# Last layer's down projection with activations stationary and 512 weight columns moving, post-norm and output with tokens on the partitions

## The chip, the cores and the metric

The kernel runs on one core of a Trainium2 chip. The metric is the time of one execution on the device in microseconds. A core has five engines that run side by side: TensorE (PE; PEld is its loading of the stationary operand), VectorE (DVE), ScalarE (ACT), GpSimd (POOL) and SyncE (SP), which here issues most of the DMA transfers. A matmul keeps a stationary 128x128 operand in the array and streams the columns of a moving operand past it.

## The reference, cut to what matters

A trunk of two layers over 16 learned meta tokens and 512 tokens of width 1024. Layer 0 mixes with attention, layer 1 with a gated DeltaNet; each is followed by a feed-forward stage. In each stage the input is normalised before, and the result is normalised again before it is added to the residual:

```python
def conv_ffn(h, w_up, conv_w, w_down):
    u = causal_dwconv(h @ w_up, conv_w)
    gate, up = jnp.split(u, [FFN_DIM], axis=-1)
    return (jax.nn.gelu(gate, approximate=True) * up) @ w_down
...
        f = conv_ffn(rmsnorm(h, norm_ffn_pre[i]), ffn_w_up[i], ffn_conv[i], ffn_w_down[i])
        h = h + rmsnorm(f, norm_ffn_post[i])
    return h[:, N_META:]
```

`rmsnorm` divides a token's row by the root of its mean square and multiplies by a gain per feature. FFN_DIM is 2816, so the down projection is 2816 by 1024; of its result only the 512 tokens are returned.

## The kernel before, in words

**Layout.** Everything lies transposed: features on the partitions (1024 features are KT = 8 tiles of 128), tokens along the free dimension. Tokens are cut in two halves; by layer 1's FFN they are 260 (the last 4 meta tokens and 256 tokens) and 256. The residual is `h[half]`, a tile of 128 x 8 x tokens.

**Precision.** Each product is computed from operands split in a high and a low part: `xh*wh + xl*wh + xh*wl`, three matmuls for each 128x128 tile of weights, accumulated in PSUM. This is `dense` (L300): the weight tile is stationary, the tokens of one half move past it, with 260 or 256 columns.

**Weights.** They come in units (`_units`, L65) laid out in DRAM in the order of use. `load` (L274) fetches a unit (at most 128 x 1024 floats) by a DMA on SP into one of two staging tiles, ACT casts it to `wh` (L285), DVE subtracts to get `wl` (L292). There are eight pairs `wh`/`wl` in this stage: six in pool `wp`, and two in `wx` for every fourth unit. `need(u)` (L295) loads units up to one ahead of `u`.

**Order.** `push(u, fn)` runs unit `u` for half 0 at once and puts half 1 off: up to six calls stay in `pending` (the lag, L1417), and the oldest is popped as a new one is pushed. `flush` runs what is left. A compile-time scheduler lays out each engine's order from these calls and modelled durations; each engine then runs its own order strictly, waiting on semaphores.

**The FFN** (`ffn`, L770) goes through 22 feature tiles of the hidden layer in blocks of FB = 7, 7, 8. An up unit makes `conv_tile` (L737): 24 matmuls, a multiplication by the pre-norm's factor (L748), three taps of the causal convolution (L755 on ACT, L764 on DVE); a gate unit adds GELU (L786), an up unit the product and its split in `ah` and `al` (L794 to L796). After a block and four units of the next, eight down units follow (`down`, L799), one for each tile of 128 output features: FB[b] x 3 matmuls for each half, and the result is copied (b = 0, on ACT) or added (L811, on DVE) to `m[half]`.

**The end.** In the last block each tile of `m` is squared on ACT (L352) and added on POOL to a running tile (L353). After the eighth, matmuls with a column of 1/D sum over the partitions (L342), DVE adds epsilon (L361), POOL takes the power -1/2 (L363), PE spreads the factors over the partitions (L365) and ACT copies them (L367). `boundary` (L402) then makes `m * gain * factor` (L411) and adds it to `h` (L412) for eight feature tiles, and a DMA on SP stores each tile (L418). Half 0 does this while half 1's last tiles run on PE; half 1 does it at the end.

Of the kernel before, what the change touches and what calls it, by code (L numbers as in the profile page):

```python
# [9 lines left out]
F32 = mybir.dt.float32  # L10
F32R = mybir.dt.float32r
BF16 = mybir.dt.bfloat16
AF = mybir.ActivationFunctionType
ALU = mybir.AluOpType
# [3 lines left out]
P = 128  # L18
D = 1024
KT = 8  # L20
NM = 16
SEQ = 512
# [4 lines left out]
FB = (7, 7, 8)  # L27
# [13 lines left out]
EPS = 1e-6  # L41
# [23 lines left out]
def _units():  # L65
    u = []
    def add(mat, layer, r0, nk, c0, M):
        u.append((mat, layer, r0, nk, c0, M))
    add("attn_w_in", 0, 0, 8, 4096, 16)
    for m in range(8):  # L70
        for s in range(4):
            add("attn_w_in", 0, 0, 8, s * 1024 + m * 128, 128)
    for m in range(8):
        add("attn_w_out", 0, 0, 8, m * 128, 128)
    def ffn(layer):
        def up(b):
            r = []
            for j in range(FB[b]):
                jj = sum(FB[:b]) + j
                r.append(("ffn_w_up", layer, 0, 8, jj * 128, 128))  # L80
                r.append(("ffn_w_up", layer, 0, 8, 2816 + jj * 128, 128))
            return r
        def down(b):
            return [("ffn_w_down", layer, sum(FB[:b]) * 128, FB[b], m * 128, 128) for m in range(8)]
        u.extend(up(0))
        for b in (1, 2):
            x = up(b)
            u.extend(x[:4]); u.extend(down(b - 1)); u.extend(x[4:])
        u.extend(down(2))
    ffn(0)  # L90
    add("dn_w_in", 0, 0, 8, -1, 40)
    for kind, g in DNSEQ:
        for hl in range(NG):
            if kind == "P":
                add("dn_w_out", 0, 0, 4, (NG * g + hl) * 128, 128)
                continue
            add("dn_w_in", 0, 0, 8, {"Q": 0, "K": 1024, "V": 2048, "H": 3072}[kind] + (NG * g + hl) * 128, 128)
    for m in range(8):
        add("dn_w_out", 0, 512, 4, m * 128, 128)
    ffn(1)  # L100
    return u


@with_exitstack
def trunk(ctx, tc, h0, wflat, params, out):
    nc = tc.nc
    pc = _param_layout()
    units = _units()
# [3 lines left out]
    HALF = [(0, 272), (272, 256)]  # L112
# [5 lines left out]
    sm = ctx.enter_context(tc.tile_pool(name="sm", bufs=1))  # L118
# [251 lines left out]
    def new_x(half, name):  # L370
        return take(half, name, F32R)


    def prenorm_tile(half, k, name, layer, xh, xl, ss):
        ss.add(h[half][:, k, :], tmp2)
        g = ng(name, layer, k)
        nc.scalar.activation(xh[:, k, :], h[half][:, k, :], AF.Identity, scale=g)
        nc.vector.scalar_tensor_tensor(xl[:, k, :], h[half][:, k, :], g, xh[:, k, :].bitcast(F32), op0=ALU.mult, op1=ALU.subtract)  # L378
# [23 lines left out]
    def boundary(half, m, ssm, post, pre):  # L402
        r = ssm.inv()
        n = HALF[half][1]
        last = pre is None
        if not last:
            xh, xl = new_x(half, "xh"), new_x(half, "xl")
            ss = SumSq(half)
        for k in range(KT):
            t = tmp2("bt")  # L410
            nc.vector.scalar_tensor_tensor(t[:, :n], m[:, k, :], ng(post[0], post[1], k), r[:, :n], op0=ALU.mult, op1=ALU.mult)  # L411
            nc.vector.tensor_tensor(h[half][:, k, :], h[half][:, k, :], t[:, :n], op=ALU.add)  # L412
            if not last:
                prenorm_tile(half, k, pre[0], pre[1], xh, xl, ss)
            else:
                s = max(HALF[half][0], NM)
                e = HALF[half][0] + n
                nc.sync.dma_start(out[:, k, s - NM:e - NM], h[half][:, k, s - HALF[half][0]:n])  # L418
        if not last:
            X[half] = (xh, xl, ss.inv())  # L420


    pending = []
# [346 lines left out]
    def ffn(layer, post, pre):  # L770
        with ExitStack() as cx:
            fp = cx.enter_context(tc.tile_pool(name="fp", bufs=1, reuse_waits="tile"))
            acts = {}
            m = [None, None]
            ssm = [None, None]
            carry = {}

            def conv(u, half, ft):
                return conv_tile(u, half, ft, 3, pc["ffn_conv"] + layer * 132, 44, fp, carry)

            gates = {}

            def gate(u, half, j):
                cv = conv(u, half, j)
                g = fp.tile([P, 272], F32, name="gl", tag="gl", bufs=3)[:, :HALF[half][1]]
                nc.scalar.activation(g, cv, AF.Gelu_apprx_tanh)  # L786
                gates[j, half] = g

            def up(u, half, j):
                n = HALF[half][1]  # L790
                cv = conv(u, half, NF + j)
                ah = fp.tile([P, 272], F32R, name="ah", tag=f"ah{half}", bufs=10)[:, :n]
                al = fp.tile([P, 272], F32R, name="al", tag=f"al{half}", bufs=10)[:, :n]
                nc.vector.tensor_tensor(cv, cv, gates.pop((j, half)), op=ALU.mult)  # L794
                nc.scalar.copy(ah, cv)
                nc.vector.tensor_tensor(al, cv, ah.bitcast(F32), op=ALU.subtract)  # L796
                acts[j, half] = (ah, al)

            def down(u, half, b, mt):  # L799
                n = HALF[half][1]  # L800
                j0 = sum(FB[:b])
                if b == 0 and mt == 0:
                    m[half] = take(half, "m")
                if b == 2 and mt == 0:
                    ssm[half] = SumSq(half)
                ps = dense(u, half, lambda k: acts[j0 + k, half][0], lambda k: acts[j0 + k, half][1])
                mm = m[half][:, mt, :]
                if b == 0:
                    nc.scalar.copy(mm, ps)
                else:  # L810
                    nc.vector.tensor_tensor(mm, mm, ps, op=ALU.add)  # L811
                if b == 2:
                    ssm[half].add(mm)
                    if mt == 7:
                        drop(*X[half][:2])
                        boundary(half, m[half], ssm[half], post, pre)
                        drop(m[half])

            def ups(b):
                r = []  # L820
                for j in range(sum(FB[:b]), sum(FB[:b + 1])):
                    r.append(lambda u, half, j=j: gate(u, half, j))
                    r.append(lambda u, half, j=j: up(u, half, j))
                return r

            def downs(b):
                return [lambda u, half, mt=mt: down(u, half, b, mt) for mt in range(8)]

            seq = ups(0)
            for b in (1, 2):  # L830
                x = ups(b)
                seq += x[:4] + downs(b - 1) + x[4:]
            seq += downs(2)
            for f in seq:
                push(nextu(), f)
            flush()
# [602 lines left out]
def _layout(inputs):  # L1439
    f = {k: np.asarray(v) for k, v in inputs.items()}  # L1440
    h = np.concatenate([f["meta_tokens"], f["x"][0]], axis=0).T
    h0 = np.ascontiguousarray(h.reshape(KT, P, T).transpose(1, 0, 2))
    parts = []
    for mat, layer, r0, nk, c0, M in _units():
        if c0 < 0:
            w = np.zeros((D, M), np.float32)
            w[:, 0:8] = f[mat][layer][:, 4096:4104]
            w[:, 32:40] = f[mat][layer][:, 4104:4112]
        else:
            w = f[mat][layer][r0:r0 + nk * P, c0:c0 + M]  # L1450
        parts.append(np.ascontiguousarray(w.reshape(nk, P, M).transpose(1, 0, 2)).reshape(-1))
    wflat = np.concatenate(parts)
    pc = _param_layout()
    prm = np.zeros((P, pc["n"]), np.float32)
    def put(name, a):
        prm[:a.shape[0], pc[name]:pc[name] + a.shape[1]] = a
    for a, b in (("mix_pre", "norm_mix_pre"), ("mix_post", "norm_mix_post"), ("ffn_pre", "norm_ffn_pre"), ("ffn_post", "norm_ffn_post")):
        put(a, f[b].reshape(16, P).T)
    put("gains", np.stack([np.concatenate([f["attn_q_norm"][0]] * 2), np.concatenate([f["attn_k_norm"][0]] * 2), f["dn_o_norm"][0]], axis=1))
    put("bf", f["attn_b_forget"][0][:, None])  # L1460
    prm[32:40, pc["alog"]] = f["dn_a_log"][0]
    prm[32:40, pc["dtb"]] = f["dn_dt_bias"][0]
    put("dn_conv", f["dn_conv"][0].reshape(4 * 24, P).T)
    put("ffn_conv", f["ffn_conv"].reshape(2 * 3 * 44, P).T)
    return {"h0": h0, "wflat": wflat, "params": prm}


# [12 lines left out]
```

## Time and profile before

| what | value |
|---|---|
| median of the runs | 1604.43 us |
| lowest and highest of 3 runs | 1603.03 and 1607.17 us |
| profiled execution: its time | 1601.35 us |
| profiled execution: its span, first to last instruction | 1599.4 us |
| mean granted TensorE clock | 0.977 |
| DMA queue of SP, share of 16 engines | 28.1% |

The span is the stretch from the first to the last instruction on record; the time includes what lies around it. In rows of the timeline, the columns are start in us, duration in us, engine, line, operation, output and inputs with their shape, count, and in brackets the engine's idle time before and what ended it. In rows of groups, busy us and the mean ns of one instruction follow the count. In rows of windows, each engine's busy time stands with its number of instructions, in the order PE, PEld, DVE, ACT, POOL, then the granted clock, the share of DMA and GB/s. Matmuls are pipelined, so a matmul's own duration (about 0.28 us) is longer than the step from one start to the next, which is what PE's time is made of.

### The profile page before, as it was taken

What the parts mean: (1) busy time and instruction counts of PE and PEld (TensorE: products, weight loads), DVE (VectorE), ACT (ScalarE), POOL (GpSimd) and SP (SyncE); (2) the same over time, 40 slices, a digit from 0 to 9 for tenths busy, and PEclk for the clock granted to TensorE, in tenths of its full rate; (3) what the DMA queues carried; (4) which work ended last, traced back from release to release, by engine and by line L of the source; (5) the groups of instructions that cost most, each with busy time, mean ns of one, the idle gap of its engine ahead of it and who ended that gap; (6) DMA issues with size and microseconds to landing.
All of it is one profiled execution on the core that took longest, in us unless ns stands there. A gap on an engine that the chain in (4) does not pass through costs nothing.

```text
span 1599.4 us, 33295 instructions
## 1 busy us (share of the span) xinstructions
PE 1525.8 (95%) x12630; PEld 1486.8 (93%) x12630; DVE 1123.4 (70%) x2629; ACT 815.4 (51%) x1925; POOL 495.8 (31%) x993
## 2 busy tenths in 40 slices
PE   8999999999999999999789899899989999999996
PEld 6999999899999999999789798898989999999996
DVE  7888888948974675674978665676569864765764
ACT  6677777735643442343564456545456543432441
POOL 6434443025300010012556475654154200100112
PEclk9999999999999999999799998999999999999998
DMA  5232222422223222222323322222141323323321
GB/s 175 89 89 79 75 78 85 134 65 82 84 83 100 93 85 88 93 93 72 107 75 90 90 61 71 68 77 61 50 150 66 91 82 106 92 82 106 93 67 53
DMA packets 63327, 139.04 MB, mean 87 GB/s; under 512 B 18584, under 2 KB 31288, under 8 KB 62784
## 3 DMA queue, kind: packets, MB, share of 16 engines
q1 hardware_dynamic: 62544, 134.55, 28.1%
q8 instruction: 99, 1.62, 0.4%
q0 software_dynamic: 480, 2.15, 0.4%
q14 instruction: 60, 0.49, 0.1%
q10 hardware_dynamic: 144, 0.22, 0.0%
HBM read 131.54 MB, written 5.36 MB: 86 GB/s over the span
## 4 chain that ended last, share of the span: by engine, by line
PE 74%; DVE 11%; POOL 5%; DMA 4%; ACT 3%; issue 3%; SPq 1%; POOLq 0%; DVEq 0%; ACTq 0%
PE ps L312 65%; POOL PR L1177 2%; POOL RB L1178 2%; DVE h L412 1%; DVE bt L411 1%; DVE wl L292 1%; PE av L698 1%; DMA w<-wflat 1%; DVE cv L764 1%; DMA gcr<-gcd 1%; PE pt L678 1%; DVE xl L378 1%; ACT wh L285 1%; PE s L1277 1%; DVE qr L577 1%
## 5 line engine op out<-in xcount | busy, mean ns | idle before, releaser
L312 PE MATMUL ps<-xh,wh 128*128 128x256 f32 (+4 forms) x2464 | 717.6, 293 | 16.8 <-DVE ub L748 9.2
L312 PE MATMUL ps<-xl,wh 128*128 128x256 f32 (+4 forms) x2464 | 710.8, 289 | 3.4 <-DVE xl L378 3.0
L312 PE MATMUL ps<-xh,wl 128*128 128x256 f32 (+4 forms) x2464 | 713.6, 290 | 0.0
L312 PEld LDWEIGHTS ps<-xh,wh 128*128 128x128 f32 (+1 forms) x2464 | 469.6, 192 | 22.8 <-DVE ub L748 6.3
L312 PEld LDWEIGHTS ps<-xl,wh 128*128 128x128 f32 (+1 forms) x2464 | 471.1, 191 | 7.4 <-DVE xl L378 4.6
L312 PEld LDWEIGHTS ps<-xh,wl 128*128 128x128 f32 (+1 forms) x2464 | 471.1, 191 | 1.0
L285 ACT CAST wh<-w 128x1024 fp32r<-128x1024 f32 (+3 forms) x226 | 225.1, 997 | 189.5 <-PE ps L312 166.7
L292 DVE TENSOR_TENSOR wl<-w,wh 128x1024 fp32r<-128x1024 f32 (+4 forms) x191 | 220.6, 1156 | 99.3 <-ACT wh L285 98.7
L764 DVE SCALAR_TENSOR_TENSOR cv<-ub,prm,cv 128x256 f32<-128x256 f32 (+2 forms) x494 | 243.8, 498 | 38.4 <-ACT cv L755 29.5
L312 PE MATMUL ps<-ah,wl 128*128 128x256 f32 (+2 forms) x704 | 199.5, 284 | 0.0
L312 PE MATMUL ps<-ah,wh 128*128 128x256 f32 (+2 forms) x704 | 199.3, 283 | 0.0
L312 PE MATMUL ps<-al,wh 128*128 128x256 f32 (+2 forms) x704 | 199.1, 283 | 0.0
L755 ACT ACTIVATE cv<-ub,prm 128x256 f32<-128x256 f32 (+2 forms) x224 | 113.8, 511 | 146.3 <-DVE ub L748 146.2
L748 DVE TENSOR_TENSOR ub<-ps,r 128x256 f32<-128x256 f32 (+2 forms) x224 | 95.4, 428 | 101.5 <-PE ps L312 100.6
L353 POOL TENSOR_TENSOR ssq<-ssq,sq 128x256 f32<-128x256 f32 (+2 forms) x98 | 90.5, 926 | 144.5 <-ACT sq L352 143.0
L312 PEld LDWEIGHTS ps<-ah,wh 128*128 128x128 f32 x704 | 132.6, 189 | 0.0
L312 PEld LDWEIGHTS ps<-al,wh 128*128 128x128 f32 x704 | 132.5, 188 | 0.0
L312 PEld LDWEIGHTS ps<-ah,wl 128*128 128x128 f32 x704 | 132.4, 188 | 0.0
L751 POOL COPY cy<-ub 128x2 f32<-128x2 f32 (+1 forms) x112 | 38.0, 341 | 279.3 <-DVE ub L748 277.7
L292 POOL TENSOR_TENSOR wl<-w,wh 128x512 fp32r<-128x512 f32 x70 | 95.0, 1377 | 72.1 <-ACT wh L285 56.8
L747 POOL COPY ub<-cy 128x2 f32<-128x2 f32 (+1 forms) x112 | 31.3, 280 | 197.1 <-DVE cv L764 160.0
L786 ACT ACTIVATE gl<-cv 128x272 f32<-128x272 f32 (+2 forms) x88 | 36.7, 418 | 42.0 <-DVE cv L764 41.7
(308 smaller groups left out, 2454.5 us busy)
## 6 DMA issues: line engine op xcount, KB each, us to landing
w<-wflat SPq DMA_DIRECT2D x176, 512.0 KB, 3.5
w<-wflat SPq DMA_DIRECT2D x32, 448.0 KB, 3.3
cB<-cdram SPq DMA_DIRECT2D x16, 264.0 KB, 3.3
w<-wflat SPq DMA_DIRECT2D x16, 256.0 KB, 2.7
h<-h SPq DMA_DIRECT2D x8, 272.0 KB, 5.3
cB<-cdram SPq DMA_DIRECT2D x16, 136.0 KB, 3.0
h<-h SPq DMA_DIRECT2D x8, 256.0 KB, 5.0
AB<-dA SPq DMA_DIRECT2D x16, 128.0 KB, 3.2
```

What stands on the lines that cost most here:

```text
L285: nc.scalar.copy(wh[:], w32)
L292: eng.tensor_tensor(wl[:, c], w32[:, c], wh[:, c].bitcast(F32), op=ALU.subtract)
L312: tok(nc.tensor.matmul(o, w[:, a], r[:, c0:c1], start=(i == 0), stop=(i == tot - 1)))
L353: nc.gpsimd.tensor_tensor(self.acc[:, :n], self.acc[:, :n], sq[:, :n], op=ALU.add)
L747: nc.gpsimd.tensor_copy(ub[:, 0:c0], carry.pop(ft)[:, :c0])
L748: nc.vector.tensor_tensor(ub[:, c0:c0 + n], ps, r[:, :n], op=ALU.mult)
L751: nc.gpsimd.tensor_copy(c[:, :c0], ub[:, n:n + c0])
L755: nc.scalar.activation(cv, ub[:, c0:c0 + n], AF.Identity, scale=w[c0])
L764: nc.vector.scalar_tensor_tensor(cv, ub[:, i:i + n], w[i], cv, op0=ALU.mult, op1=ALU.add)
L786: nc.scalar.activation(g, cv, AF.Gelu_apprx_tanh)
L1177: nc.gpsimd.tensor_tensor(t, R3[:, 0:a, l:l + 1].to_broadcast([P, a, w]), A3[:, l:l + 1, l + 1:32].to_broadcast([P, a, w]), op=ALU.mult)
L1178: nc.gpsimd.tensor_tensor(R3[:, 0:a, l + 1:32], R3[:, 0:a, l + 1:32], t, op=ALU.subtract)
```

## The change: what it does

Layer 1's down projection is turned. The activations `ah` and `al` of 128 tokens are stationary, and 512 columns of weights move; the result has tokens on the partitions and output features along the free dimension. The 512 tokens are four blocks of 128 (half 0 drops its 4 meta tokens). Down units hold two rows of tiles by 512 columns; block b has two groups (f = 0 and 1, the two halves of the output features) of four units each, as many units and bytes as before.

`down_rows(b, f)` takes all four units of its group. It pops what is pending, one call after each `need`, so the half-1 calls of the ups are drained ahead of a block's first group; it also loads the four units that follow. Then for each of the four token blocks it runs FB[b] x 3 matmuls of 512 columns into one PSUM bank, and copies (b = 0, ACT) or adds (DVE) it to `m[half]`, now a tile of 128 tokens x 2 x 1024.

In the last block ACT squares the row with a sum along the free dimension (`accum_out`), DVE multiplies by the gain, which a DMA has spread over all partitions from a new input `gpost`; in the first group `turn_h` transposes the residual's block by eight PE transpositions (fp32, 128x128) into two banks, which ACT copies. After the second group DVE adds the two sums and epsilon, POOL takes the power, and DVE makes `m * factor + h` in two pieces of 512 columns, each stored by a DMA of 256 KB. `boundary` loses its last-layer branch, and the output's layout is (128, 4, 1024).

```diff
         def down(b):
+            if layer == 1:
+
+                return [("ffn_w_down", layer, (sum(FB[:b]) + k) * 128, min(2, FB[b] - k), f * 512, 512) for f in range(2) for k in range(0, FB[b], 2)]
             return [("ffn_w_down", layer, sum(FB[:b]) * 128, FB[b], m * 128, 128) for m in range(8)]
...
+            def turn_h(half, tb):
+                if tb == 0:
+                    W["h", half] = take(half, "hT", shape=[P, 2, D])
+                c = HALF[half][1] - 256 + tb * 128
+                for kk in range(2):
+                    pt = psum_tile()
+                    for k in range(4):
+                        nc.tensor.transpose(pt[:, k * 128:k * 128 + 128], h[half][:, kk * 4 + k, c:c + 128], ident[:])
+                    nc.scalar.copy(W["h", half][:, tb, kk * 512:kk * 512 + 512], pt[:])
+
+            def down_rows(b, f):
+                us = [nextu() for _ in range((FB[b] + 1) // 2)]
+                for u in us:
+                    need(u)
+                    if pending:
+                        a, fn = pending.pop(0)
+                        fn(a, 1)
+                while pending:
+                    a, fn = pending.pop(0)
+                    fn(a, 1)
+                    need(us[-1] + 4 - len(pending), 0)
+                need(us[-1] + 4, 0)
+                if b == 0 and f == 0:
+                    for half in range(2):
+                        m[half] = take(half, "m", shape=[P, 2, D])
+                if b == 2 and f == 0:
+                    for half in range(2):
+                        drop(*X[half][:2])
+                    W["g"] = take(0, "gb", shape=[P, D])
+                    nc.sync.dma_start(W["g"][:], gpost[0:1, :].to_broadcast([P, D]))
+                    W["s"] = sm.tile([P, 16], F32, name="rst", tag="rst")
+                fs = slice(f * 512, f * 512 + 512)
+                j0 = sum(FB[:b])
+                for t in range(4):
+                    half, tb = t // 2, t % 2
+                    c = HALF[half][1] - 256 + tb * 128
+                    ps = psum_tile()
+                    for k in range(FB[b]):
+                        wh, wl, nk, M = loaded[us[k // 2]]
+                        a = slice(k % 2 * 512, k % 2 * 512 + 512)
+                        ah, al = (x[:, c:c + 128] for x in acts[j0 + k, half])
+                        for i, (x, w) in enumerate(((ah, wh), (al, wh), (ah, wl))):
+                            nc.tensor.matmul(ps[:], x, w[:, a], start=(k == 0 and i == 0), stop=(k == FB[b] - 1 and i == 2))
+                    mm = m[half][:, tb, fs]
+                    if b == 0:
+                        nc.scalar.copy(mm, ps[:])
+                    else:
+                        nc.vector.tensor_tensor(mm, mm, ps[:], op=ALU.add)
+                    if b < 2:
+                        continue
+
+                    st = W["s"]
+                    nc.scalar.activation(ps[:], mm, AF.Square, scale=D ** -0.5, accum_out=st[:, 4 * f + t:4 * f + t + 1])
+                    nc.vector.tensor_tensor(mm, mm, W["g"][:, fs], op=ALU.mult)
+                    if f == 0:
+                        turn_h(half, tb)
+                        continue
+                    nc.vector.tensor_scalar(st[:, 8 + t:9 + t], st[:, t:t + 1], st[:, 4 + t:5 + t], EPS, op0=ALU.add, op1=ALU.add)
+                    nc.gpsimd.tensor_tensor(st[:, 12 + t:13 + t], st[:, 8 + t:9 + t], mhalf[:, 0:1], op=ALU.pow)
+                    for i in range(2):
+                        o = m[half][:, tb, i * 512:i * 512 + 512]
+                        nc.vector.scalar_tensor_tensor(o, o, st[:, 12 + t:13 + t], W["h", half][:, tb, i * 512:i * 512 + 512], op0=ALU.mult, op1=ALU.add)
+                        nc.sync.dma_start(out[:, t, i * 512:i * 512 + 512], o)
+
+            if layer == 1:
+                def put(fs):
+                    for f in fs:
+                        push(nextu(), f)
+                put(ups(0))
+                for b in range(2):
+                    x = ups(b + 1)
+                    put(x[:4])
+                    for f in range(2):
+                        down_rows(b, f)
+                    put(x[4:])
+                for f in range(2):
+                    down_rows(2, f)
+                return
```

More of the change, by code (lines that the diff above doesn't have):

```diff
@@ L104, in trunk @@
 @with_exitstack
-def trunk(ctx, tc, h0, wflat, params, out):
+def trunk(ctx, tc, h0, wflat, params, gpost, out):
     nc = tc.nc
@@ L404, in boundary @@
         n = HALF[half][1]
[L405 to L408, printed above, removed]
+        xh, xl = new_x(half, "xh"), new_x(half, "xl")
+        ss = SumSq(half)
         for k in range(KT):
@@ L412, in boundary @@
             nc.vector.tensor_tensor(h[half][:, k, :], h[half][:, k, :], t[:, :n], op=ALU.add)
[L413 to L420, printed above, removed]
+            prenorm_tile(half, k, pre[0], pre[1], xh, xl, ss)
+        X[half] = (xh, xl, ss.inv())
     pending = []
@@ L827, in downs @@
                 return [lambda u, half, mt=mt: down(u, half, b, mt) for mt in range(8)]
+            W = {}
+            def turn_h(half, tb):
[7 more added lines that the diff above has]
+                    nc.scalar.copy(W["h", half][:, tb, kk * 512:kk * 512 + 512], pt[:])
@@ L1464, in _layout @@
     put("ffn_conv", f["ffn_conv"].reshape(2 * 3 * 44, P).T)
-    return {"h0": h0, "wflat": wflat, "params": prm}
+    gpost = np.ascontiguousarray(f["norm_ffn_post"][1][None, :])
+    return {"h0": h0, "wflat": wflat, "params": prm, "gpost": gpost}
 def kernel(**inputs):
@@ L1473 @@
     args = [nc.dram_tensor(n, a.shape, mybir.dt.from_np(a.dtype), kind="ExternalInput").ap() for n, a in arrays.items()]
-    o = nc.dram_tensor("out", (P, KT, SEQ), F32, kind="ExternalOutput").ap()
+    o = nc.dram_tensor("out", (P, SEQ // P, D), F32, kind="ExternalOutput").ap()
     with tile.TileContext(nc, schedule_with_timeline_sim=True) as tc:
@@ L1478 @@
     got = r.results[0]["out"]
-    return np.ascontiguousarray(got.transpose(2, 1, 0).reshape(1, SEQ, D))
+    return np.ascontiguousarray(got.transpose(1, 0, 2).reshape(1, SEQ, D))
```

## The prediction, made before the run

> **What bounds the kernel now.** I read the page first: how busy each engine is and which engine holds the chain that ended last.
>
> ```profile
> span 1599.4 us, 33295 instructions
> PE 1525.8 (95%) x12630; PEld 1486.8 (93%) x12630; DVE 1123.4 (70%) x2629; ACT 815.4 (51%) x1925; POOL 495.8 (31%) x993
> PE 74%; DVE 11%; POOL 5%; DMA 4%; ACT 3%; issue 3%; SPq 1%; POOLq 0%; DVEq 0%; ACTq 0%
> ```
>
> TensorE is the bound on average, but the change sits in one stage, layer 1's FFN. So next come the chain of waits in order of time for that stage, and the busy times of a stretch of mixed up and down projections.
>
> ```profile
> 1232.80 339.35 PE ps L312 x2843
> 1572.15 0.56 PE psn L342 x6
> 1576.26 0.33 PE psn L365 x3
> 1300.00:1400.00 100.00, 100.00 (x840) 100.00 (x839) 57.44 (x103) 41.66 (x77) 6.46 (x32) 1.00 0.32 95
> 1380.00:1403.00 23.00, 23.00 (x195) 23.00 (x194) 18.02 (x37) 10.81 (x20) 2.72 (x12) 1.00 0.29 86
> ```
>
> From 1232.8 to 1572 us nothing but matmuls is on the path; PE never waits, at full granted clock. The 840 matmuls in 100 us give the pitch now, 119.05 ns for a mean of 258 moving columns. Only what changes PE's own stream, or the tail behind it, can move the end. The tail, from the timeline:
>
> ```profile
> 1585.66 0.28 PE L312 MATMUL ps<-ah,wl 128*128 128x256 f32 x1
> 1585.98 0.42 DVE L811 TENSOR_TENSOR m<-m,ps 128x256 f32<-128x256 f32 x1 [0.93 <-PE ps L312]
> 1586.50 0.42 ACT L352 ACTIVATE sq<-m 128x256 f32<-128x256 f32 x1 [1.27 <-DVE m L811]
> 1587.06 0.72 POOL L353 TENSOR_TENSOR ssq<-ssq,sq 128x256 f32<-128x256 f32 x1 [0.95 <-ACT sq L352]
> 1587.83 0.61 PE L342 MATMUL psn<-oneD,ssq 128*128 128x1 f32 x4 [1.89 <-POOL ssq L353]
> 1588.48 0.16 DVE L361 TENSOR_SCALAR nst<-psn 128x2 f32<-128x2 f32 x1 [2.07 <-PE psn L342]
> 1588.72 0.71 POOL L363 TENSOR_TENSOR nst<-nst,mhalf 128x2 f32<-128x2 f32 x1 [0.94 <-DVE nst L361]
> 1589.48 0.43 PE L365 MATMUL psn<-ident,nst 128*128 128x128 f32 x2 [1.04 <-POOL nst L363]
> 1589.95 0.37 ACT L367 COPY r<-psn 128x256 f32<-128x256 f32 x1 [3.03 <-PE psn L365]
> 1590.35 2.07 DVE L411 SCALAR_TENSOR_TENSOR bt<-m,prm,r 128x256 f32<-128x256 f32 x5 [1.72 <-ACT r L367]
> 1595.20 1.09 DVE L412 TENSOR_TENSOR h<-h,bt 128x256 f32<-128x256 f32 x3
> ```
>
> Last matmul start to end of span: 1599.40 - 1585.66 = 13.7 us, nearly six of them sixteen VectorE operations of the post-norm, which needed every output tile's sum of squares first.
>
> **Term 1, the matmul pitch.** The down projection goes from 22 x 3 x 8 x 2 = 1056 matmuls of 260 or 256 columns to 22 x 3 x 4 x 2 = 528 of 512. The columns streamed hardly fall (272,448 to 270,336), so the gain must come from whatever a matmul costs beyond its columns. The trace has no 512-column matmul here; it has runs of 24 at 256 and at 272 columns (first and last start of each, 23 steps), and three instructions in a row, two of 400 columns.
>
> ```profile
> 438.51 0.28 PE L312 MATMUL ps<-xh,wh 128*128 128x256 f32 x1
> 441.26 0.28 PE L312 MATMUL ps<-xh,wl 128*128 128x256 f32 x1
> 447.29 0.28 PE L312 MATMUL ps<-xh,wh 128*128 128x272 f32 x1
> 450.19 0.29 PE L312 MATMUL ps<-xh,wl 128*128 128x272 f32 x1
> 97.64 0.34 PE L646 MATMUL sc<-KS,QS 128*128 128x400 f32 x1
> 97.82 0.34 PE L647 MATMUL sc<-KS,QZ 128*128 128x400 f32 x1
> 98.00 0.23 PE L649 MATMUL sc<-cmask,identb 128*128 128x128 bf16 x1
> ```
>
> Steps: 2.75/23 = 119.6 ns at 256, 2.90/23 = 126.1 at 272, 180 at 400. From 256 to 400 a column costs 60.4/144 = 0.42 ns, leaving about 12 ns per matmul that does not grow. At 512: 180 + 112 x 0.42 = 227 ns. Then 1056 x 0.11905 = 125.7 us becomes 528 x 0.227 = 119.9: **-5.8 us**. Ends: no excess at all at 512, 0.42 x 512 = 215 ns (-12.2 us); cost proportional to columns, 126.1/272 x 512 = 237 ns (-0.6). I take the slope because the 400-column row lies on it and is nearest.
>
> The Trainium skill (TensorE: Matmul & The Clock Gate, Back-to-back issue gap) puts the isolated gap at N/2.4 + 2.5 ns, 109 at 256 columns and 216 at 512. The trace disagrees at 256 (119.6) and 400 (180 against 169); with its 216 at 512 against the measured 119.05 the term would be -11.7 us.
>
> **Term 2, norm work inside the stream.** Half 0's sum reduction and its transpositions back leave PE: 0.56 + 0.33 = **-0.9 us**, from the chain's rows above.
>
> **Term 3, h is turned.** turn_h adds 4 blocks x 8 = 32 fp32 transpositions to PE's stream. One such transposition among 272-column matmuls:
>
> ```profile
> 105.70 0.29 PE L312 MATMUL ps<-xh,wh 128*128 128x272 f32 x1
> 105.83 0.27 PE L666 MATMUL pt<-ident,S 128*128 128x128 f32 x1
> 105.85 0.37 PE L312 MATMUL ps<-xl,wh 128*128 128x272 f32 x1
> 106.06 0.29 PE L312 MATMUL ps<-xh,wl 128*128 128x272 f32 x1
> ```
>
> Two matmul steps take 0.252 us; here they take 0.36, so a transposition costs 0.11 us: **+3.5 us**, ends 0 and 32 x 0.27 = 8.6, the record's own length if nothing overlapped. It waits for h, long there, and a PSUM bank of the six. Its eight ACT copies, 512 columns each, are hidden: ACT is busy 42 of 100 us. Uncovered they would cost one copy, 0.6 us, per bank waited for.
>
> The Trainium skill (TensorE: Matmul & The Clock Gate, Part 4: PE-mode transpose) speaks against this step with about 275 ns per transpose in a kernel. The record's 0.27 agrees, the step of 0.11 does not; by the page the term would be 8.8 us.
>
> **Term 4, drains and restarts.** A ten-microsecond stretch of layer 0's FFN start, the nearest likeness of a restart, stands first; then what a weight unit costs VectorE, ScalarE and the DMA, and an output piece:
>
> ```profile
> 375.00:385.00 10.00, 9.45 (x75) 9.12 (x74) 9.93 (x14) 4.56 (x11) 7.18 (x6) 1.00 0.46 156
> L292 DVE TENSOR_TENSOR wl<-w,wh 128x1024 fp32r<-128x1024 f32 x141 | 173.9, 1234 | 81.6 <-ACT wh L285 81.3
> L285 ACT CAST wh<-w 128x1024 fp32r<-128x1024 f32 x176 | 184.3, 1049 | 138.3 <-PE ps L312 121.2 <-DMA w<-wflat 14.5 <-PE psn L365 0.2
> w<-wflat SPq DMA_DIRECT2D x176, 512.0 KB, 3.5
> out<-h SPq DMA_DIRECT2D x16, 128.0 KB, 1.8
> ```
>
> Until now ups of half 0 and lagging work of half 1 alternate all through the stage. Now the six pending half-1 calls are drained ahead of each block's downs, and after two blocks the ups restart with half 0 alone. In a drain, DVE does per half-unit: 18.02 us over 23 us, which is 4 units of 48 matmuls at 0.119, is 4.5 per unit, less one 1.2 us subtraction, halved, 1.65; plus a subtraction, since each popped call frees a buffer: 2.85 us, against 24 x 0.119 = 2.86 of PE. It keeps up barely, with six PSUM banks as slack, and the downs behind it ask little of DVE. A group holds four of the eight wh/wl pairs and the next group's four are loaded meanwhile: four chains in 84 x 0.227 = 19 us, 4 x 1.2 of DVE; that covers them. The casts wait on ACT's queue for those buffers, and down evictions or squares may queue behind; PSUM banks cover that too. The restart loads three units in six half-units. I take 0.55 us idle for each of two restarts: **+1.1 us**, ends 0 and 6. The gain's broadcast DMA waits on SP for X's slot; no weight load is behind it, and DVE's product with the gain, which waits for it, holds only the evictions of block 2, first wanted 5 us into the group. The evictions, four per group where there were sixteen per block of half the width, are hidden behind the next block's 4.8 us of matmuls; so are six of the eight output DMAs, which follow all weight loads on SP.
>
> **Term 5, the tail.** Three durations at 512 columns and the accumulator's read:
>
> ```profile
> L681 DVE TENSOR_TENSOR PTLB<-pt,PTHB 128x512 fp32r<-128x512 f32 x16 | 11.1, 692 | 5.7 <-ACT PTHB L680 5.5
> L680 ACT CAST PTHB<-pt 128x512 fp32r<-128x512 f32 x16 | 9.2, 576 | 15.8 <-PE pt L678 15.8
> L653 ACT ACTIVATION_READ_ACCUMULATOR S<-S,st 128x1 f32 x80 | 15.1, 188 | 0.0
> ```
>
> From the last matmul's start: 0.32 as now plus 0.107 for 256 more columns; add 0.69; gap 0.1; Square 0.58 + 0.19; gap 0.1; product with the gain 0.69 (it overwrites what Square reads, so it cannot run beside it); the small add 0.16; gap 0.1; POOL pow 0.71; gap 0.1; two 512-wide operations 2 x 0.69. That is 5.2 us. Now the last VectorE end, 1596.29, to the end is 3.1 us; the out piece doubles to 256 KB, and by the two DMA rows 128 KB costs (3.5 - 1.8)/3 = 0.57. Tail 5.2 + 3.7 = 8.9 against 13.7: **-4.8 us**. Ends: -6 (small add first, product beside the pow) and -2.5 (a piece landing in 3.5 us, slower operations).
>
> **Sum:** -5.8 - 0.9 + 3.5 + 1.1 - 4.8 = -6.9 us. The profiled execution took 1601.35 us (span 1599.4, 1.95 around it) and would take 1594.4; it lies 3.1 below the median 1604.43 of the runs, from which the forecast is **1597.5 us**.
>
> **Rivals.** *No excess at 512* (chance 0.14): the 12 ns are pressure of the weight load, which a longer stream hides. For: PEld is as busy as PE. Against: 400 columns still shows it. 215 ns: -13.3 in all, 1591.1 us. The Trainium skill's gap rule, quoted under term 1 (TensorE: Matmul & The Clock Gate, Back-to-back issue gap), belongs here.
>
> *Proportional pitch* (0.12): 237 ns, total -1.7, 1602.7 us. For: 119.6/256 and 126.1/272 are 0.467 and 0.464. Against: 180/400 is 0.45.
>
> *Transpositions not overlapped* (0.05): 0.27 us each, +5.1, 1602.6 us. Against: the step of 0.11. The Trainium skill's 275 ns, quoted under term 3 (TensorE: Matmul & The Clock Gate, Part 4: PE-mode transpose), belongs here.
>
> *Slower, late weights* (0.10): a down group holds its four pairs until its last block, so at five borders (between a block's two groups, and before each restart) the next weights may start only there. A whole chain is 3.5 + 1.05 + 1.23 = 5.8 us; five exposed are 29 us, 1626; half covered, 1612. It decides once a border costs over 1.4 us, and over 2.4 makes it slower by over 0.3%. For: ACT's casts already wait for PE. Against: eight pairs hold two groups, and DMA is 32% busy.
>
> That the change does not do what it says is hardly open: operand order and width stand in the call.
>
> **Numbers.** Forecast 0.59, rivals 0.14, 0.12, 0.05, 0.10. A measurement tells about 0.3%, 4.8 us, from no change. The forecast case passes that mostly: 0.49 of its 0.59, and with the first rival 0.63; the two flat rivals and the rest of the forecast give 0.26, late weights 0.11. The range reaches from inside the first rival, 1589, to 1606, past the flat ones.
>
> **What would show it.** Right: 512-column steps near 227 ns, the down groups gapless, 0.11 us per transposition, under 10 us from last matmul to end. Wrong: PE idle at L312's successor with ACT or DVE wl as releaser at group borders; steps of 215 or 237; a tail above 11 us.

## The result, and the profile after

The changed kernel takes 1596.16 us in the median of 6 runs (1591.6 to 1599.85), the kernel before 1604.08 us on the same chip; the ratio is 0.9945, with a 95% interval of 0.9925 to 0.9965. The forecast was 1597.5 us, 6.9 us less than the 1604.43 of the three runs known then; the two medians here lie 7.9 us apart. The profiled execution of the changed kernel took 1593.63 us, its span 1591.9 us.

From the page after, the same three lines as before:

```profile
span 1591.9 us, 32178 instructions
PE 1525.3 (96%) x12119; PEld 1462.9 (92%) x12119; DVE 1114.2 (70%) x2599; ACT 815.7 (51%) x1923; POOL 489.6 (31%) x981
PE 70%; DVE 10%; POOL 8%; issue 4%; ACT 4%; DMA 3%; SPq 1%; POOLq 0%; DVEq 0%; ACTq 0%
```

PE has 511 matmul records fewer and is busy for 0.5 us less. So the fewer and wider matmuls, together with the transpositions that came with them, have bought hardly anything on PE; the 7.5 us by which the span is shorter must lie elsewhere. The chain of waits of the last stage shows where (start, length, what):

```profile
1231.54 77.42 PE ps L315 x647
1308.96 39.07 PE ps L870 x168
1348.03 80.39 PE ps L315 x672
1428.42 39.03 PE ps L870 x168
1467.45 68.88 PE ps L315 x576
1536.33 5.55 PE ps L870 x24
1541.88 0.87 PE ps L835 x8
1542.76 5.56 PE ps L870 x24
1548.32 0.87 PE ps L835 x8
1549.19 5.61 PE ps L870 x24
1554.80 0.87 PE ps L835 x8
1555.67 5.58 PE ps L870 x24
1561.25 0.87 PE ps L835 x8
1562.12 16.74 PE ps L870 x72
```

The piece at 1231.54 is the one that began at 1232.80 before. The pieces join without a gap: each ends where the next one starts, so the drains, the four-unit groups and the restarts of the ups cost no idle time. Rows of L870 are the new down projection, 168 matmuls in 39.07 us, 232.6 ns each; rows of L835 are the transpositions, eight in 0.87 us.

The tail, from the timeline:

```profile
1584.05 0.39 PE L870 MATMUL ps<-wl,ah 128*128 128x512 f32 x1
1584.48 0.69 DVE L875 TENSOR_TENSOR m<-m,ps 128x512 f32<-128x512 f32 x1 [1.18 <-PE ps L870]
1585.26 0.60 ACT L880 ACTIVATE ps<-m 128x512 f32<-128x512 f32 x1 [4.87 <-DVE m L875]
1585.79 0.19 ACT L880 ACTIVATION_READ_ACCUMULATOR ps<-m 128x1 f32 x1
1586.01 0.69 DVE L881 TENSOR_TENSOR m<-m,gb 128x512 f32<-128x512 f32 x1 [0.85 <-ACT ps L880]
1586.62 0.21 DVE L885 TENSOR_SCALAR rst<-rst 128x1 f32<-128x1 f32 x1
1586.91 0.54 POOL L886 TENSOR_TENSOR rst<-rst,mhalf 128x1 f32<-128x1 f32 x1 [5.05 <-DVE rst L885]
1587.48 1.41 DVE L889 SCALAR_TENSOR_TENSOR m<-m,rst,hT 128x512 f32<-128x512 f32 x2 [0.66 <-POOL rst L886]
```

From the last matmul's start to the end of the span it is 1591.9 - 1584.05 = 7.85 us; before it was 13.7.

So the stage is accounted for. From the start of that first piece to the last matmul's start: 352.9 us before (1232.80 to 1585.66), 352.5 us after (1231.54 to 1584.05). PE's stream is 0.35 us shorter, the tail 5.9 us. The other 1.3 us of the 7.5 lie ahead of the stage; up to the first down unit of layer 1, or the load of its weights, the two programs give every engine the same instructions in the same order, and in the kernels below that are also alike up to there or to the stage's start, that piece began anywhere between 1228.1 and 1238.0 us. That is the scatter of the earlier stages, and it is why the profiles are compared here from that piece on.

### The profile page after: what moved, and what is told of

The parts are those of the page before. It is cut to its first block, busy times and chain, and to the rows that moved or that the text cites. A ratio compares the mean times of both kernels' runs of the same rounds, so it can differ in the third digit from the quotient of the medians.

```text
span 1591.9 us, 32178 instructions
## 1 busy us (share of the span) xinstructions
PE 1525.3 (96%) x12119; PEld 1462.9 (92%) x12119; DVE 1114.2 (70%) x2599; ACT 815.7 (51%) x1923; POOL 489.6 (31%) x981
## 4 chain that ended last, share of the span: by engine, by line
PE 70%; DVE 10%; POOL 8%; issue 4%; ACT 4%; DMA 3%; SPq 1%; POOLq 0%; DVEq 0%; ACTq 0%
PE ps L315 55%; PE ps L870 7%; POOL PR L1255 3%; POOL RB L1256 3%; DVE h L413 1%; DVE wl L295 1%; PE av L693 1%; DVE bt L412 1%; PE pt L673 1%; DVE xl L381 1%; DVE cv L759 1%; DMA AB<-dA 1%; ACT wh L288 1%; DVE qr L572 1%; PE sc L641 1%
## 5 line engine op out<-in xcount | busy, mean ns | idle before, releaser
L356 POOL TENSOR_TENSOR ssq<-ssq,sq 128x256 f32<-128x256 f32 (+2 forms) x84 | 79.1, 945 | 109.2 <-ACT sq L355 107.7
L315 PE MATMUL ps<-ah,wl 128*128 128x256 f32 (+1 forms) x352 | 100.3, 285 | 0.0
L315 PE MATMUL ps<-ah,wh 128*128 128x256 f32 (+1 forms) x352 | 100.2, 285 | 0.0
L315 PE MATMUL ps<-al,wh 128*128 128x256 f32 (+1 forms) x352 | 100.0, 285 | 0.0
L742 POOL COPY ub<-cy 128x2 f32<-128x2 f32 (+1 forms) x112 | 35.1, 313 | 176.8 <-DVE cv L759 145.1
L870 PE MATMUL ps<-wh,ah 128*128 128x512 f32 x176 | 69.9, 397 | 0.0
L870 PE MATMUL ps<-wh,al 128*128 128x512 f32 x176 | 69.4, 394 | 0.0
L870 PE MATMUL ps<-wl,ah 128*128 128x512 f32 x176 | 69.4, 394 | 0.0
L315 PEld LDWEIGHTS ps<-al,wh 128*128 128x128 f32 x352 | 66.4, 189 | 0.0
```

The costliest lines, as they stand in the source:

```text
L315: tok(nc.tensor.matmul(o, w[:, a], r[:, c0:c1], start=(i == 0), stop=(i == tot - 1)))
L356: nc.gpsimd.tensor_tensor(self.acc[:, :n], self.acc[:, :n], sq[:, :n], op=ALU.add)
L742: nc.gpsimd.tensor_copy(ub[:, 0:c0], carry.pop(ft)[:, :c0])
L870: nc.tensor.matmul(ps[:], x, w[:, a], start=(k == 0 and i == 0), stop=(k == FB[b] - 1 and i == 2))
```

## The experiments

Theory after the result: PE's stream bounds the last stage and stayed as long as it was, what the wide matmuls saved being spent on the transpositions; the gain is the bare tail, the stretch behind PE's last matmul that nothing overlaps. Rival: the stream is what became shorter. "The stage" below runs from the start of the chain's piece of 647 up matmuls to the end of the span: 366.6 us in the kernel before, from its piece at 1232.80; 1591.9 - 1231.54 = 360.4 in the changed kernel.

**The changed kernel once more**, with no edit.

> The changed kernel once more, as the yardstick for the runs beside it. Theory: the gain is the tail (last matmul to end 13.7 us before, 7.85 us after, 5.9 us less), while PE's stream of the last stage stays as long as it was (512-column matmuls at 232 ns: 528 x 0.232 = 122.7 against 125.7 us, minus 3.0; norm work minus 0.9; 32 transpositions plus 3.5). So 6 us faster than the kernel before, give or take the scatter of the earlier stages. Rival: the stream is what became shorter, and the 1.4 us by which the last stage began earlier in the profile belongs to the change; then about 8 us.

Measured: 1598.33 us (median of 12) against 1603.09, ratio 0.9964 (0.9945 to 0.9983). Its profile has the stage at 1593.4 - 1233.05 = 360.35 us and the tail at 7.84. In these two profiles the stage repeats within 0.1 us while the twelve runs scatter by 12 us, so the stage's 6.2 us are what the change is worth; both intervals hold that (0.9961). They do not shut out the rival's 8 us, but the stage's start does: it came at 1233.05 here, later than the 1232.80 of the kernel before, so the earlier start of the first profile was scatter.

**Two matmuls of 256 columns for each of 512.**

```diff
+                            for q in range(0, 512, 256):
+                                nc.tensor.matmul(ps[:, q:q + 256], x, w[:, a.start + q:a.start + q + 256], ...)
```

> Each 512-column matmul of the down projection becomes two of 256 columns on the same stationary activations, into the two halves of the same bank; the turn, the order and the tail stay. Theory (stream bound, 119 ns at 256 and 232 at 512): 528 x (2 x 0.119 - 0.232) = 3.2 us slower than the changed kernel, about 1599, and still about 4 us faster than the kernel before, since the tail is kept. Rival (the width makes the gain): about 6 to 8 us slower than the changed kernel, no gain left. Second rival (a matmul pays only for its columns): no difference.

Measured: 1598.75 us, ratio 0.9978 (0.9959 to 0.9998); the interval overlaps that of the kernel run beside it, so the time alone does not tell them apart. The profile does. Its chain:

```profile
1234.38 77.42 PE ps L315 x647
1311.81 39.77 PE ps L871 x336
```

336 matmuls in 39.77 us are 118.4 ns each, 236.7 for two against 232.6 for one; the stage takes 1597.0 - 1234.38 = 362.6 us, 2.3 more than the changed kernel's. The theory holds, a little below its 3.2: width is worth two to three microseconds, and without it the stage is still 4 us shorter than before.

**No transpositions.** The output lacks the residual.

```diff
-                        turn_h(half, tb)
...
-  W["h", half][:, tb, i * 512:i * 512 + 512]
+  W["g"][:, i * 512:i * 512 + 512]
```

> The 32 transpositions of the residual and their eight copies are left out; the last operation adds the gain tile in place of the turned residual, so the output lacks the residual. Theory: 8 transpositions take 0.87 us of PE's stream, which is the bound, so 3.5 us faster than the changed kernel, about 1592.7. Rival (the copies and the bank waits cost more than the transpositions): 5 us or more. Second rival (hidden): no difference.

Measured: 1592.38 us, ratio 0.9938 (0.992 to 0.9956). The stage takes 1594.9 - 1237.98 = 356.9 us, 3.5 less than the changed kernel's: the transpositions cost their full 4 x 0.87 us, and nothing else was late.

**All transpositions ahead of the stage.**

```diff
-                        turn_h(half, tb)
...
+                for half in range(2):
+                    for tb in range(2):
+                        turn_h(half, tb)
+                    drop(h[half])
                 put(ups(0))
```

> The same 32 transpositions, moved ahead of the first up unit of the last stage, where PE is idle for about 6 us while VectorE works through the boundary (54.5 us busy of 60 in the kernel before); the residual tiles are given back afterwards. Theory: they fall into that idle time, and the whole 3.5 us come back: about 1592.7. Rival: their ACT copies and PSUM banks hold up the boundary and the first ups, and the gain is under 1 us or turns into a loss of up to 3 us.

Measured: 1604.47 us, ratio 0.9999 (0.9982 to 1.0016): the whole gain of the change is gone, 6.1 us more than the changed kernel beside it took. The expectation was wrong in place and size, its rival, a loss of up to 3 us, in size. The ten microseconds from 1200 of the window view, first of this kernel and then of the unedited one (the changed kernel run again, in whose profile VectorE's work at the boundary lies 5.1 us later), and what PE waited for most in this kernel (us in all, times, longest):

```profile
1200.00:1210.00 10.00, 4.44 (x17) 2.85 (x18) 9.86 (x20) 6.86 (x17) 3.81 (x5) 0.50 0.17 52
```

```profile
1200.00:1210.00 10.00, 10.00 (x68) 10.00 (x67) 9.93 (x16) 5.59 (x14) 4.65 (x5) 0.76 0.47 148
```

```profile
PE ps L835 <- DVE h L413: 10.2, 7, 2.9
```

PE was not idle there before in the sense that counts: it was working off the ups of half 0 while VectorE was still making the residual. In this kernel it stood 10.2 us at transpositions, issuing 17 instructions where there had been 68, at a granted clock of 0.50. Whose transpositions these were, the timeline tells:

```profile
1201.21 0.69 PE L835 MATMUL ps<-ident,h 128*128 128x128 f32 x2 [2.94 <-DVE h L413]
1205.35 0.84 DVE L413 TENSOR_TENSOR h<-h,bt 128x260 f32<-128x260 f32 x1
1208.32 0.69 PE L835 MATMUL ps<-ident,h 128*128 128x128 f32 x2 [1.38 <-DVE h L413]
1210.26 0.57 PE L315 MATMUL ps<-xh,wh 128*128 128x260 f32 x1
```

VectorE's last addition to half 0 (260 columns) starts at 1205.35. Six of the seven waits, 8.8 us, end with additions to half 0; only the last, 1.38 us, is for half 1. What the edit did is to lay the ups behind all of half 0's transpositions and the first of half 1's: PE's first up matmul starts 17.3 us after VectorE's first addition to h (1192.98), against 1.8 in the unedited kernel (1199.89 after 1198.10). PE takes its instructions in order, so the ups that could have run stood behind the waiting transpositions. From VectorE's last addition to the first down unit it is 99.8 us, against 85.7; the 3.5 us of the turn come back at the end. Why the ups were laid so late no run separates. The kernel's code points to the six PSUM banks as much as to the order of the calls: the eight turned blocks are asked for first and take the banks in rotation, so the first up gets a bank that ScalarE frees only by its copies of half 0, the first of which starts at 1205.41.

**Only half 0 turned early.**

```diff
-                        turn_h(half, tb)
+                        if half == 1:
+                            turn_h(half, tb)
...
+                for tb in range(2):
+                    turn_h(0, tb)
+                drop(h[0])
                 put(ups(0))
```

> Only half 0's residual (16 of the 32 transpositions) is turned ahead of the last stage's first up unit; half 1's stays in the last block. Turned wholly ahead, PE stood for 10.2 us at transpositions that waited for VectorE to finish half 1's residual, with the ups of half 0 queued behind them, and the last stage's stream began to fill some 14 us late. Theory (the loss came from half 1's place in PE's strict order): without half 1's part the ups run as in the changed kernel, and 1.75 us of PE's stream come back, so 0 to 2 us faster than the changed kernel. Rival (the loss came from the copies on ScalarE and the PSUM banks at the boundary): about half of the loss stays, 2 to 4 us slower than the changed kernel.

Measured: 1595.41 us, ratio 0.9938 (0.9918 to 0.9958), in time no different from the changed kernel. In the profile VectorE ended the boundary as in the unedited kernel (its last addition to h at 1224.84 against 1224.73 us), but the first down matmul came at 1314.37 instead of 1310.47. From that addition it is 3.8 us later than in the unedited kernel's profile, and 2.3 later than in that of the kernel with 256 columns, whose clock was lower behind the boundary (see the last section). 1.75 us were saved at the end, as the same 1.75 us of transpositions now stand ahead; that leaves a net loss of 0.5 to 2.0 us. PE's first up came 1.8 us after VectorE's first addition again, and it still waited for a residual:

```profile
PE psn L345 <- POOL ssq L356: 4.0, 1, 4.0
PE ps L835 <- DVE h L413: 3.0, 3, 1.1
PE ps L315 <- DVE xl L381: 0.2, 1, 0.2
```

So 7 of the 10.2 us of waiting went when half 1's part was left out, although most of them had been waits for half 0: now the ups run between half 0's transpositions, of which three groups still wait, 3.0 us in all. The expectation starts from waits for half 1, which the rows above do not show. By the profile its theory, a gain of up to 2 us, did not come, and the loss is at most at the low end of the rival's 2 to 4. No run separates what the ScalarE copies and the banks add. Neither of the two edits found a free place on PE for the turn at the stage's start.

**bf16 operands for the down projection.** Both parts of activations and weights are bf16, so the products carry about 16 bits.

```diff
-                ah = fp.tile([P, 272], F32R, name="ah", ...)
+                ah = fp.tile([P, 272], BF16 if layer == 1 else F32R, name="ah", ...)
...
-        wh = pool.tile([P, n], F32R, name="wh", tag="wh")
+        wh = pool.tile([P, n], BF16 if bf else F32R, name="wh", tag="wh")
```

> The down projection's operands (high and low parts of the activations and of the weights) are held as bf16 instead of 32-bit floats, so the products carry about 16 bits; all else as in the changed kernel. It asks what the 232 ns of a 512-column matmul are made of: the steps at 256, 272 and 512 columns lie on 0.443 ns per column plus 5.5. Theory: the slope above 0.417 comes with the four-byte operands; then the step falls to 213 to 219 ns, 528 matmuls take 7 to 10 us less, about 1588 to 1591. Rival: the slope has nothing to do with the operands' width; the step stays at 232 and the time within 1 us of the changed kernel's stage.

Measured: 1587.0 us, ratio 0.9903 (0.9878 to 0.9929). From its chain:

```profile
1230.03 77.42 PE ps L316 x647
1307.45 36.28 PE ps L872 x168
```

36.28/168 = 216.0 ns instead of 232.6; the stage is 1581.7 - 1230.03 = 351.7 us, 8.7 less than the changed kernel's, and 528 x 16.6 ns = 8.8. The theory holds, with a step in the middle of its 213 to 219 ns and a time 1 us below its range: 16.6 of the 232.6 ns come with the four-byte operands. Whether with the moving or the stationary one this run does not tell, since both were changed.

**Four matmuls of 128 columns**, the edit of the 256 with `128` in its place.

> Each 512-column matmul becomes four of 128 columns on the same stationary activations. Theory: below some 250 columns a step is set by the load of the stationary operand, which is issued for each matmul, at about 116 ns (the steps of 144-column matmuls in the kernel before); 2112 x 0.116 = 245 us instead of 123, so about 1716. Rival (a step costs its columns plus 5.5 ns): 2112 x 0.062 = 131 us, about 1602.

Measured: one run, 1710.44 us. From its chain:

```profile
1235.34 77.42 PE ps L315 x647
1312.76 74.99 PE ps L871 x672
```

74.99/672 = 111.6 ns, not 62: at 128 columns a step is not set by its columns. That fits the load of the stationary operand, which each matmul issues, as the floor, but no run varies that load alone, so it is not shown; the step lies 7 ns below the one at 256.

**A shorter tail.** The product with the gain goes to a tile of its own in half 1; the last block's 512 columns are computed as two banks of 256, and its last two output pieces are 256 columns wide.

```diff
-                    nc.vector.tensor_tensor(mm, mm, W["g"][:, fs], op=ALU.mult)
+                    pr = W["p"] if half == 1 else m[half]
+                    nc.vector.tensor_tensor(pr[:, tb, fs], mm, W["g"][:, fs], op=ALU.mult)
...
+                    if b == 2 and f == 1 and t == 3:
+                        last_rows(us, j0, c)
+                        continue
...
+                for q in range(2):
+                    ps = psum_tile()
...
+                    s = slice(512 + q * 256, 768 + q * 256)
...
+                for s in (slice(0, 512), slice(512, 768), slice(768, 1024)):
```

> Nothing but the tail is changed: the product with the gain goes to a tile of its own, so that it runs beside Square; the last block's 512 columns are computed as two banks of 256, so that the first one's add, Square and product lie under the second one's matmuls; the last output piece is 256 columns. Theory (the tail is bare, every us of it is a us of the time): 0.7 for the product, 0.45 for the narrower add and Square, 0.6 for the smaller last piece, less 0.1 for 24 matmuls split in two: last matmul to end about 6.2 us instead of 7.85, 1.6 us faster. Rival (the end is set by the queue of output DMAs, not by the chain of engines): no difference.

Measured: 1596.64 us, ratio 0.9947 (0.9928 to 0.9965), not told from the changed kernel in time. In the profile the last matmul starts at 1585.09 and the span is 1591.7, a tail of 6.6 us, 1.24 shorter. VectorE's and ScalarE's part of it:

```profile
1585.41 0.42 DVE L851 TENSOR_TENSOR m<-m,ps 128x256 f32<-128x256 f32 x1 [0.68 <-PE ps L848]
1585.87 0.42 DVE L853 TENSOR_TENSOR pr<-m,gb 128x256 f32<-128x256 f32 x1
1585.87 0.39 ACT L852 ACTIVATE ps<-m 128x256 f32<-128x256 f32 x1 [1.38 <-DVE m L851]
```

Product and Square now start together, which is the 0.7 of the expectation; its 0.6 for the smaller last piece did not come, as the end still came 2.9 us after VectorE's last operation (3.0 in the changed kernel). The whole stage is 1591.7 - 1233.21 = 358.5 us, 1.9 shorter: beside the tail the stream lost 0.6, most of it in the ups, which the edit does not touch and which ran a little faster (the piece of 647 took 77.25 us, not 77.42). The same 0.17 us stand in the next kernel, which has this edit too; the cause is open.

**Both**, the last two edits of the down projection together (bf16 operands, short tail).

> The short tail and the bf16 operands of the down projection together. If the two theories hold, the parts add up: 8 to 12 us faster than the changed kernel and 14 to 18 us faster than the kernel before, about 1587; if only the tail is bare, 1.6 us faster than the changed kernel.

Measured: 1583.29 us, ratio 0.988 (0.9851 to 0.9909). The stage is 1578.3 - 1228.14 = 350.2 us, 10.2 less than the changed kernel's: 8.7 and 1.24, and 0.3 beside, of the size of the faster ups. It beats both kernels. It also has a run of bf16 matmuls of 256 columns, 47 steps from the first to the last of these two:

```profile
1566.49 0.27 PE L850 MATMUL ps<-wh,ah 128*128 128x256 bf16 x1
1571.62 0.27 PE L850 MATMUL ps<-wl,ah 128*128 128x256 bf16 x1
```

5.13/47 = 109.1 ns at 256 columns in bf16.

**Both, with half 0 turned early.**

> The bf16 operands of the down projection, the short tail and half 0 turned early, together. Theory: like the first two together (0.988 of the kernel before) and 0 to 2 us less, 0.987. Rival: 2 to 4 us more, 0.990.

Measured: 1584.87 us, ratio 0.9873 (0.9854 to 0.9893), not told from the kernel without the turn. It shows nothing beyond what the run with half 0 alone showed.

## Why the prediction was right, and where it was not

The time, the sign and the size came out (1596.2 against 1597.5; the stage 6.2 us shorter against 6.9), but the two largest terms were off in opposite directions: term 1 gained 2.9 us less than forecast, the terms 4 and 5 together 2.2 more. That the sum came so close is in part luck.

**Term 1, the matmul pitch: mis-sized.** The step that failed is "I take the slope because the 400-column row lies on it and is nearest". The measured step at 512 is 232.6 ns, not 227, and the term -2.9 us (528 x 0.2326 = 122.8 against 125.7), half of -5.8. (The step before is 339.35/2843 = 119.4 ns by the chain's row; the 119.05 counts matmuls that reach over the window's edges too. With 119.4 the term is -3.2.) The 400-column rows were two single steps, written to 10 ns and next to instructions of other kinds; 119.6 at 256 and 232.6 at 512 give 0.44 ns a column and about 7 ns beside it, where I had put 0.42 and 12. That line has 183 ns at 400, which two such rows can't tell from 180. The proportional rival (237), given a chance of 0.12, is nearer to 232.6 than the 227 that was taken. The rival without any excess at 512 (215) is refuted for four-byte operands, and the bf16 run shows under what condition it is true: 109.1 ns at 256 and 216.0 at 512.

The Trainium skill's N/2.4 + 2.5 for the isolated gap (TensorE: Matmul & The Clock Gate, Back-to-back issue gap) gives 109 and 216 for these two widths. The trace agrees to 0.3 ns with bf16 operands and disagrees by 9 and 17 ns with the four-byte operands of this kernel.

**Terms 2 and 3** held. The norm work is gone from the stream, and with the three other terms as measured, -2.9 - 0.9 + 3.5 + 0 = -0.3, the stream's -0.35 is met; with -3.2 it is met within 0.3. The transpositions cost 0.109 us each in a run of eight against 0.11 predicted, and leaving them out gave back 3.5 us. The rival that priced them at their record's 0.27 is refuted.

**Term 4, drains and restarts**, was 1.1 us and measured 0. The late-weights rival is refuted by the gapless chain. The cover was better than the one named: the second group's weights were ready by 1310.66, when the first group had hardly begun (1308.96), and the four units of ups for the restart at 1348.03 by 1335.59.

**Term 5, the tail**, was -4.8 and measured -5.9, by two rows above all: POOL's power of one column, 0.54 against 0.71, and the output piece of 256 KB, which ended the span 3.0 us after VectorE, not 3.7, and so no later than the piece of 128 KB did before (3.1). That Square holds back the product with the gain, which overwrites what it reads, was right: L881 starts when Square's read ends, and the shorter tail shows it by removing it.

**What the sum hid.** I counted on the stream for 2.1 of 6.9 us. It gave 0.35. The change's name speaks of activations stationary and 512 columns moving; what it is worth, as I read the two tails, is that with tokens on the partitions a row's sum of squares falls out of one ScalarE instruction, and that only one block of 128 tokens is left to finish when PE stops, instead of half of the tokens over all features. Splitting the matmuls again lost 2.3 us of the 6.2, taking the turn away added 3.5 to them. No run takes the two parts of the tail, the sum of squares and the single block, apart.

## What to carry to other kernels

Where one engine is busy without a gap, price a change in its steps, start to start, and take the step from the same kind of instruction at the nearest size, over a long run: here a slope taken from two rows rounded to 10 ns put a term off by a factor of two, since the term is a small difference of large times. Look at the end of the last engine in the chain as a term of its own; a layout in which the last piece can be finished alone was worth twice the wider matmuls. Before moving work to where an engine looks idle, ask what it waits for, what is queued behind it and which buffers it holds meanwhile: in a strict order, an instruction that waits takes along all those that could have run. And see in the timeline for which tile it waited before naming the culprit.

## What the runs showed of the hardware that was not expected

A matmul of 512 columns took 232.6 ns with four-byte operands and 216.0 in bf16, one of 256 columns 118.4 and 109.1, at a granted clock of 1.00 in all of these stretches; at 128 columns with four-byte operands the step was 111.6. The bf16 operands, without any other change, are worth more here than the whole change under study (8.7 against 6.2 us of the stage).

The same 37 matmuls at the head of the last stage, right behind PE's wait for the boundary, took 4.7 us in five profiles, that of the kernel before among them, and 6.2 in four others, so that the stage's true start differs by 1.5 us among runs of like code:

```profile
1223.40 4.68 PE ps L315 x37
```

```profile
1223.20 6.21 PE ps L315 x37
```

The first is the changed kernel run again, the second the one with 256 columns. Over the first stretch the granted clock was 1.00, over the second 0.73, which accounts for the difference. The Trainium skill (TensorE: Matmul & The Clock Gate, Part 1: The HAM clock gate) describes a free-running window of activity after which an idle PE is slowed, so that the phase decides; no run here shows the window itself.
